# Two-layer recurrent decoder step on one core: second feed-forward's right operands formed inside the residual tiles, pools placed by hand, one store on another queue

## Chip, cores, metric

The kernel runs on one core of a Trainium2 chip. The metric is the device time of one execution in microseconds; several executions are timed and their median is quoted. One more execution is profiled, and all rows below come from that one.

## What is computed

T = 1048 columns are carried through a trunk of two layers: 16 meta tokens and 1024 prompt tokens (one sequence, 1040 columns) and 8 single-token samples. The model width is 1024, so the residual is eight tiles of 128 x 1048. The reference, cut to what matters here:

```
for layer in range(2):
    x = even_mixer(x, ...) if layer == 0 else odd_mixer(x, ...)
    x = conv_ffn(x, buf_ffn[layer], norm_ffn[layer], w_up[layer], ..., w_down[layer])
y = rmsnorm(x, norm_final)

def conv_ffn(x, buf, norm, w_up, conv_w, conv_b, w_down):
    hup = rmsnorm(x, norm) @ w_up                  # 1024 -> 2 x 2816
    gate, val = jnp.split(hup, 2, axis=-1)
    gate, new_buf = causal_dwconv(gate, buf, conv_w, conv_b)   # width 3 over time
    return x + (jax.nn.gelu(gate) * val) @ w_down, new_buf     # 2816 -> 1024

def rmsnorm(x, g):
    return x * lax.rsqrt(jnp.mean(x * x, axis=-1, keepdims=True) + EPS) * g
```

The layer-0 mixer holds a gated linear attention and a diagonal state-space model. The layer-1 mixer is a Griffin block: a gelu branch times a gated linear recurrence, then an output projection of 1536 to 1024 that is added to x.

## The kernel before

Names: X0 to X7 are the residual tiles, HALF = 524 columns is half of one. PE does the matmuls, DVE, ACT and POOL are the three elementwise engines, SP issues most of the DMAs, POOL issues some. The kernel names its engines V (DVE), A (ACT) and P (POOL), and `tt` is a tensor_tensor on DVE unless P is given as its last argument. All queues run in order; a tile scheduler has laid out the order of each engine's instructions from the program text, and pools (stacks of tiles) decide which tile lies where in SBUF. A tile that is put where another lay waits for all readers and writers of that other.

**Split products.** Each float32 matmul operand is split into a high part (`split`: an ACT cast, L85) and a low part (the difference, on DVE, L45); a product is three matmuls (`mm3`, L128 to L130).

**Feed-forward, up.** `ffn_up` makes the two 2816-wide outputs in 22 inner tiles (`hidden(t)`, t = 0 to 21). It takes the 2 x 2 blocks (rows of x in two groups of four tiles, columns in two halves of 524) through seven products, not eight. The class `Seven` prepares the right operands from x times its gain: B11, B21, T2, T3, T1, B22 and T4, each for j = 0 to 3 (pair Xj, Xj+4). B11, B21 and B22 are quarters of x themselves (`plain`), and the other four are running differences (`sums`): ACT scales four quarters into tiles t of a pool of three (`t7`, L1013), POOL makes four subtractions per j, and each result is split. The left operands are sums of weight blocks (`sums(t)` in `ffn_up`): four blocks are loaded into wA (SP), POOL adds and subtracts them into wS, and the four results are split (whi, wlo). In `hidden(t)` the order of products is B11, B21, then T2, T3, T1, B22, T4. B11 and B21 of tiles 0 and 1 need no differences, and are made first for both (`first`), and between them and the rest stands `nx.finish()`, which sums the squares over partitions by an all-ones matmul (L147) and makes RB, the reciprocal root-mean-square. PSUM results go to p1 and R (B11 plus B21), u2 and u4 (kept partial sums), VL and C; VL is stored to DRAM as hdr[t] at L1186.

**Feed-forward, down.** `ffn_down` loads hdr[t] back as hr (L1216), splits it (ph, pl) and multiplies by the down weights in turns of 2, 4, 4, 4, 4, 4 inner tiles. A turn has 24 output pieces (8 tiles of x, 3 column ranges); each takes one of four PSUM banks ("bank") and is added to X by DVE, which frees the bank. At the start, X is loaded back from the DRAM copy xdn (L1224), issued by POOL.

**Layer-1 mixer.** Eight steps, two column halves by four groups G. The output projection `out` of one step runs in the next; the last one (`end`) adds to X column half 1 and calls `after` for each finished piece: sums of squares (`stats`, ACT squares, POOL adds into acc), the store of X to xdn (POOL queue), and for j = 0 to 2 the `sums` and B22. The operands B11 and B21 are made in the step half 1, G = 2; sums of j = 3 come after the mixer's pools are closed. Then `ffn_up(1)` begins.

So there are four places where one stage hands over to the next and PE depends on the other engines: mixer 0 to feed-forward 0 (about 535 to 575 us), up to down in layer 0 (994 to 1016), mixer 1 to feed-forward 1 (1756 to 1825), up to down in layer 1 (2244 to 2275).

The seven lines of `hidden` on which much below rests:

```
p1_ = [fp.tile([128, H2], F32, name="p1", bufs=2) for _ in range(2)]
R = fp.tile([128, 2 + T], F32, name="R", tag="rvc", bufs=5)
...
P.memset(R[:, 0:2], 0.0)
...
put(R, 2, p1, W)
...
prod(Z, ws2, "T2", False)
```

## Time and profile before

| what | value |
|---|---|
| median of 3 runs | 2531.71 us (2529.97 to 2532.13) |
| the profiled execution's own time | 2529.29 us |
| its span, first to last instruction | 2527.4 us |
| mean granted PE clock | 0.975 of full speed |
| busy share of the span | PE 94%, DVE 72%, ACT 45%, POOL 25% |

The span is what the views of the trace cover; 1.9 us of the profiled execution's time lie around it. PE's idle time, the span less its busy time, is 161.5 us in all; most of the kernel is a stretch in which PE never waits, and the idle time sits at the places listed above and inside the mixers.

### The profile page before, as it was taken

To read this page: it belongs to the slowest core of one execution; us is meant where nothing else is said; L and a number is where in the kernel's file an instruction comes from. 1 tells how busy PE (TensorE), PEld (TensorE's weight loads), DVE (VectorE), ACT (ScalarE), POOL (GpSimd) and SP (SyncE) were. 2 spreads that over 40 slices of the span, in tenths; PEclk is the share of its full clock that TensorE was granted. 3 is DMA by queue.
4 is the path that set the end of the run, shared out by engine and by line. 5 is a ranking of instruction groups with operands and counts; after the bars stand their busy time and mean duration, and the time that the engine had idled before them with its cause. 6 is when DMAs were issued, how large, how long until landed. Compare 5 with 4: busy or idle time off the path is not lost. (4 is left out here: it accounts for less than half of the span.)

```text
span 2527.4 us, 45164 instructions
## 1 busy us (share of the span) xinstructions
PE 2365.9 (94%) x17427; PEld 2318.0 (92%) x17427; DVE 1811.7 (72%) x3199; ACT 1133.1 (45%) x2258; POOL 620.4 (25%) x637
## 2 busy tenths in 40 slices
PE   7879999889999997999999999999499999979998
PEld 6778988879999997999999999999499999979998
DVE  9885788697777775654688778777777777755445
ACT  5124563654444443221575666657444444432123
POOL 4330000373333332000220001112644334310003
PEclk9999999999999999999999999999799999999999
DMA  3422325633333334332123333234233333343321
GB/s 116 106 70 79 101 79 168 205 112 114 120 122 121 119 115 146 125 106 90 46 85 96 99 100 93 87 101 136 99 116 120 114 114 114 119 169 115 96 85 69
DMA packets 200703, 277.08 MB, mean 110 GB/s; under 512 B 34312, under 2 KB 114136, under 8 KB 200488
## 3 DMA queue, kind: packets, MB, share of 16 engines
q1 hardware_dynamic: 189000, 254.43, 31.6%
q0 software_dynamic: 4736, 17.32, 1.9%
q10 hardware_dynamic: 6752, 2.45, 0.4%
q8 instruction: 137, 2.24, 0.4%
q14 instruction: 78, 0.64, 0.1%
HBM read 216.69 MB, written 51.43 MB: 106 GB/s over the span
## 5 line engine op out<-in xcount | busy, mean ns | idle before, releaser
L85 ACT CAST whi<-wraw 128x512 fp32r<-128x512 f32 (+2 forms) x449 | 261.3, 589 | 509.4 <-PE bank L129 384.8
L45 DVE TENSOR_TENSOR wlo<-wraw,whi 128x512 fp32r<-128x512 f32 (+2 forms) x448 | 330.3, 743 | 106.1 <-ACT whi L85 91.9
L45 DVE TENSOR_TENSOR X<-X,bank 128x352 f32<-128x352 f32 (+4 forms) x436 | 211.8, 489 | 226.2 <-PE bank L130 223.6
L128 PE MATMUL bank<-ph,whi 128*128 128x352 f32 (+1 forms) x960 | 311.1, 325 | 28.1 <-ACT ph L85 24.6
L129 PE MATMUL bank<-pl,whi 128*128 128x352 f32 (+1 forms) x960 | 311.5, 324 | 0.0
L130 PE MATMUL bank<-ph,wlo 128*128 128x352 f32 (+1 forms) x960 | 310.3, 323 | 0.0
L45 POOL TENSOR_TENSOR acc<-acc,sq 128x352 f32<-128x352 f32 (+3 forms) x105 | 112.9, 1082 | 591.9 <-ACT sq L143 589.3
L45 DVE TENSOR_TENSOR wlo<-wS,whi 128x512 fp32r<-128x512 f32 x176 | 126.7, 721 | 141.0 <-ACT whi L85 140.6
L85 ACT CAST whi<-wS 128x512 fp32r<-128x512 f32 x176 | 109.0, 621 | 251.1 <-PE p L129 143.7
L128 PEld LDWEIGHTS bank<-ph,whi 128*128 128x128 f32 x960 | 181.9, 190 | 29.9 <-ACT ph L85 25.5
L129 PEld LDWEIGHTS bank<-pl,whi 128*128 128x128 f32 x960 | 181.9, 189 | 1.3 <-DVE pl L45 0.5
L130 PEld LDWEIGHTS bank<-ph,wlo 128*128 128x128 f32 x960 | 182.0, 190 | 0.0
L45 POOL TENSOR_TENSOR wS<-wA 128x512 f32<-128x512 f32 x88 | 150.8, 1714 | 119.7 <-DVE wlo L45 112.3
L128 PE MATMUL bank<-H,whi 128*128 128x352 f32 (+1 forms) x480 | 160.8, 338 | 19.0 <-DVE X L45 9.0
L129 PE MATMUL bank<-L,whi 128*128 128x352 f32 (+1 forms) x480 | 160.2, 336 | 6.8 <-DVE L L48 6.6
L130 PE MATMUL bank<-H,wlo 128*128 128x352 f32 (+1 forms) x480 | 157.9, 331 | 0.9 <-DVE wlo L45 0.9
L45 POOL TENSOR_TENSOR wS<-wA,wS 128x512 f32<-128x512 f32 x44 | 57.5, 1308 | 372.6 <-DVE wlo L45 372.6
L48 DVE SCALAR_TENSOR_TENSOR C<-R,CV,C 128x1040 f32<-128x1040 f32 x88 | 132.9, 1510 | 0.6 <-ACT C L1176 0.6
L128 PEld LDWEIGHTS bank<-H,whi 128*128 128x128 f32 x480 | 93.1, 195 | 23.3 <-DVE X L45 9.4
L128 PE MATMUL bank<-ryh,whi 128*128 128x262 f32 x372 | 105.5, 286 | 3.1 <-ACT ryh L85 1.8
L129 PE MATMUL bank<-ryl,whi 128*128 128x262 f32 x372 | 105.6, 285 | 0.6 <-DVE ryl L45 0.6
L130 PE MATMUL bank<-ryh,wlo 128*128 128x262 f32 x372 | 105.2, 284 | 0.0
(807 smaller groups left out, 8229.3 us busy)
## 6 DMA issues: line engine op xcount, KB each, us to landing
wA<-in_w_up SPq DMA_DIRECT2D x176, 256.0 KB, 2.7
wraw<-in_w_up SPq DMA_DIRECT2D x132, 256.0 KB, 4.8
wraw<-in_w_in SPq DMA_DIRECT2D x96, 256.0 KB, 2.6
hdr<-VL SPq DMA_DIRECT2D x44, 524.0 KB, 4.0
hr<-hdr SPq DMA_DIRECT2D x44, 524.0 KB, 3.9
wraw<-in_w_dn SPq DMA_DIRECT2D x80, 256.0 KB, 2.6
wraw<-in_w_out SPq DMA_DIRECT2D x48, 256.0 KB, 2.7
xdn<-X POOLq DMA_DIRECT2D x16, 524.0 KB, 3.8
```

What stands on the lines that cost most here:

```text
L45: return (eng or V).tensor_tensor(out=o, in0=x, in1=y, op=op)
L48: V.scalar_tensor_tensor(out=o, in0=x, scalar=s, in1=y, op0=op0, op1=op1)
L85: A.copy(out=h, in_=x)
L128: PE.matmul(out=out, lhsT=wh, rhs=xh, start=first and i == 0, stop=False, **kw)
L129: PE.matmul(out=out, lhsT=wh, rhs=xl, start=False, stop=False, **kw)
L130: PE.matmul(out=out, lhsT=wl, rhs=xh, start=False, stop=last and i == n - 1, **kw)
```

## The change

1. `Seven` has two new methods. `gained` scales a half of X in place by its gain (ACT). `sums_in` forms the differences in place in Xj and Xj+4: two subtractions per j on POOL and two on DVE where `sums` had four on POOL, and five splits. Layer 1 uses these; the pool t7 is gone, and j = 3 is treated like the others.
2. In the last three steps but one of mixer 1, a new `before(m)` does for the first column half of tile m: stats, its store to xdn, `gained`, and the split that makes B11 or B21. `after` now stores and scales only the second half, then calls `sums_in`. Since `gained` overwrites X, it waits until the store of that half has landed.
3. The pools of `ffn_up` are laid out by `places`, R, VL and C have two buffers each where they shared five, and `nx.finish()` stands inside `hidden(0)` behind the T2 product.
4. The store of the last inner tile, hdr[21], is issued by POOL, not by SP.
5. In `ffn_down`, every other piece of the first turn takes its PSUM bank from the ring "aux", so eight banks serve it; some tiles are padded.

```
...
-                    self.o[k, j] = tuple(pool.tile([128, HALF], F32R, name=f"{k}{j}{x}") for x in "hl")
+                    hl = pool.tile([128, 2, HALF], F32R, name=f"{k}{j}")
+                    self.o[k, j] = hl[:, 0], hl[:, 1]
...
+        def gained(self, m, x):
+            A.activation(out=x, in_=x, func=ACTF.Copy, scale=CV[:, self.gain + m:self.gain + m + 1])
+        def sums_in(self, j, x1, x2):
+            a0, a1 = slice(0, HALF), slice(HALF, T)
+            tt(x1[:, a0], x1[:, a1], x1[:, a0], SUB, P)
+            split(*self.o["B22", j], x2[:, a1])
+            tt(x1[:, a1], x2[:, a1], x1[:, a1], SUB, P)
+            tt(x2[:, a1], x2[:, a1], x1[:, a0], SUB)
+            split(*self.o["T2", j], x2[:, a1])
+            split(*self.o["T3", j], x1[:, a1])
+            split(*self.o["T1", j], x1[:, a0])
+            tt(x2[:, a0], x2[:, a0], x2[:, a1], SUB)
+            split(*self.o["T4", j], x2[:, a0])
...
-        es, fp = open_pool(f"ffn{layer}")
+        es = ExitStack()
+        at = {}
+        def places(name, *tags):
+            at.update(dict.fromkeys(tags, es.enter_context(tc.tile_pool(name=f"{name}{layer}", bufs=1, reuse_waits="tile"))))
+        if fw:
+            at.update(wA=fw, wS=fw)
+            places("fa", "p1", "R")
+            places("fb", "VL", "C", "u2", "u4", "FC")
+        else:
+            places("fa", "wA")
+            places("fb", "VL", "u2")
+            places("fc", "wS")
+            places("fd", "C", "u4", "FC")
+            places("fe", "p1", "R")
+        fp = at["FC"]
...
-                r[i, k] = (fw or fp).tile([128, 512], F32, name="wA", bufs=4)
+                r[i, k] = at["wA"].tile([128, 512], F32, name="wA", bufs=4)
-            s1, s2, s3, s4_ = ((fw or fp).tile([128, 512], F32, name="wS", bufs=3) for _ in range(4))
+            s1, s2, s3, s4_ = (at["wS"].tile([128, 512], F32, name="wS", bufs=3) for _ in range(4))
...
-            p1_ = [fp.tile([128, H2], F32, name="p1", bufs=2) for _ in range(2)]
-            R = fp.tile([128, 2 + T], F32, name="R", tag="rvc", bufs=5)
+            p1_ = [at["p1"].tile([128, H2], F32, name="p1", bufs=2) for _ in range(2)]
+            R = at["R"].tile([128, 2 + T], F32, name="R", bufs=2)
...
-                    u = p1_[c] if nm == "p1" else fp.tile([128, H2], F32, name=nm, bufs=2)
+                    u = p1_[c] if nm == "p1" else at[nm].tile([128, H2], F32, name=nm, bufs=2)
...
-            VL = fp.tile([128, T], F32, name="VL", tag="rvc", bufs=5)
+            VL = at["VL"].tile([128, T], F32, name="VL", bufs=2)
+            if t == 0:
+                nx.finish()
...
-            C = fp.tile([128, T], F32, name="C", tag="rvc", bufs=5)
+            C = at["C"].tile([128, T], F32, name="C", bufs=2)
...
-            nc.sync.dma_start(out=hdr[t], in_=VL)
+            (P if t == NFF - 1 else nc.sync).dma_start(out=hdr[t], in_=VL)
-        nx.finish()
...
-        def place(t):
-            return tuple(dq.tile([128, T], F32R, name=f"{x}{t % 6}") for x in ("ph", "pl"))
-        places = {t: place(t) for t in ((2, 3) if nxt else (2, 3, 4, 5))}
+        def place(t, pad=0):
+            hl = (dq.tile([128, T + pad], F32R, name=f"{x}{t % 6}") for x in ("ph", "pl"))
+            return tuple(x[:, :T] for x in hl)
+        places = {t: place(t, 136 if nxt and t == 3 else 0) for t in ((2, 3) if nxt else (2, 3, 4, 5))}
-            dl = [tuple(dq.tile([128, 512], F32R, name=f"{x}{m}") for x in ("wh", "wl")) for m in range(8)]
+            dl = [tuple(dq.tile([128, 512 if m < 7 else 768], F32R, name=f"{x}{m}") for x in ("wh", "wl")) for m in range(8)]
...
-            for m, (c0, n) in order:
+            for i, (m, (c0, n)) in enumerate(order):
-                p = bank()
+                p = ps.tile([128, 512], F32, name="p", tag="aux", bufs=4) if t0 == 0 and i % 2 else bank()
...
-            P.dma_start(out=xdn[m], in_=X[m])
-            if 4 <= m < 7:
-                nxt.sums(m - 4, X[m - 4], X[m], t7)
-                nxt.plain(m - 4, X[m], "B22")
+            P.dma_start(out=xdn[m][:, HALF:], in_=X[m][:, HALF:])
+            nxt.gained(m, X[m][:, HALF:])
+            if m >= 4:
+                nxt.sums_in(m - 4, X[m - 4], X[m])
+    def before(m):
+        for c0, n in HCH:
+            stats(m, c0, n)
+        P.dma_start(out=xdn[m][:, :HALF], in_=X[m][:, :HALF])
+        nxt.gained(m, X[m][:, :HALF])
+        op = "B11" if m < 4 else "B21"
+        nxt.o[op, m % 4] = halves(hlp, 0, m)
+        split(*nxt.o[op, m % 4], X[m][:, :HALF])
...
-    early = [(m, c0, n) for m in range(8) for c0, n in HCH]
...
-        if half and G == 2:
-            for i, op in enumerate(("B11", "B21")):
-                for j in range(4):
-                    nxt.o[op, j] = halves(hlp, 0, 4 * i + j)
-                    nxt.plain(j, X[4 * i + j], op)
-                for _ in range(6):
-                    if early:
-                        stats(*early.pop(0))
+                for m in range(3 * G, min(3 * G + 3, 8)):
+                    before(m)
-    t7s, t7 = open_pool("t7")
-    nxt.new(range(3), ("T1", "B22", "T4"), bm)
+    nxt.new(range(4), ("T1", "B22", "T4"), bm)
-    t7s.close()
-    bls, bl = open_pool("bl1", "right")
+    xps.close()
-    nx.new((3,), ("T1", "B22", "T4"), bl)
-    t7s, t7 = open_pool("t7")
-    nx.sums(3, X[3], X[7], t7)
-    nx.plain(3, X[7], "B22")
-    t7s.close()
-    xps.close()
-    bls.close()
```

What the change moves, as each engine's instructions stand in program order. Numbers in names tell tiles apart; b0 to b3 are T2, b4 to b7 T3 of j = 0 to 3, and l and h the low and high part.

DVE at the hand-over to feed-forward 1, before: the last splits of the differences, then the first work on R, then the weight sums' low parts. t_20851 is a tile of t7.

```order
L45 TENSOR_TENSOR T13l<-t_20851,T13h 128x524
L48 SCALAR_TENSOR_TENSOR B223l<-X_11447,CV,B223h 128x524
L45 TENSOR_TENSOR T43l<-t_20851,T43h 128x524
L45 TENSOR_TENSOR R<-p_20880,p 128x262
L45 TENSOR_TENSOR R<-p_20881,p 128x262
L45 TENSOR_TENSOR R<-p_20952,p 128x262
L45 TENSOR_TENSOR R<-R,RB 128x524
L45 TENSOR_TENSOR R<-p_20953,p 128x262
L156 RECIPROCAL RB<-RB 128x262 x2
L45 TENSOR_TENSOR wlo<-wS,whi 128x512 x3
```

The same place after; X_11423 is X7, X_11419 X3, T_20458 and T_20466 are T1 and T4 of j = 3, B_20462 is B22 of j = 3.

```order
L45 TENSOR_TENSOR B_20462<-X_11423,B_20462 128x524
L45 TENSOR_TENSOR T_20465<-X_11422,T_20465 128x524
L45 TENSOR_TENSOR X_11423<-X_11423,X_11419 128x524
L45 TENSOR_TENSOR b7l<-X_11419,b7h 128x524
L45 TENSOR_TENSOR T_20458<-X_11419,T_20458 128x524
L45 TENSOR_TENSOR b3l<-X_11423,b3h 128x524
L45 TENSOR_TENSOR X_11423<-X_11423 128x524
L156 RECIPROCAL RB<-RB 128x262
L45 TENSOR_TENSOR T_20466<-X_11423,T_20466 128x524
L156 RECIPROCAL RB<-RB 128x262
L45 TENSOR_TENSOR R<-R,RB 128x524 x2
L45 TENSOR_TENSOR wlo<-wS,whi 128x512 x4
```

The four pieces of R now stand further up, between the splits; subtractions into X7 have come in; both products of R with RB stand in front of the weight splits.

ACT at the same place after: the last cast of a difference, and then two first taps of the convolution, C, ahead of the casts of the weight sums (before, the casts of the sums came first).

```order
L85 CAST T43_20466<-X7_11423 128x524
L1213 ACTIVATE C_21175<-R_20843,CV_69 128x524
L1213 ACTIVATE C_21364<-R_20915,CV_69 128x524
L85 CAST whi_21000<-wS_20994 128x512
```

SP where feed-forward 0 goes from up to down, before:

```order
L113 DMA wraw_11727<-in_w_dn 128x2x128
L113 DMA wraw_11793<-in_w_dn 128x4x128
L1186 DMA hdr21_5007<-VL_11277 128x1048
L1216 DMA hr_11487<-hdr0_4986 128x1048
L1216 DMA hr_11497<-hdr1_4987 128x1048
```

POOL at that place after, whose queue held only the loads of X there before:

```order
L1223 DMA hdr21_5007<-VL_11252 128x1048
L1262 DMA X0_11416<-xdn0_4978 128x1048
L1262 DMA X1_11417<-xdn1_4979 128x1048
L1262 DMA X2_11418<-xdn2_4980 128x1048
```

The store has left SP, where the two loads of hr now follow the weights directly, and stands on POOL ahead of all loads of X. Layer 1 has the same orders at its place.

## Rows read from the trace of the kernel before

**Rows 1.** View 1 of the page, busy time by engine.

```profile
PE 2365.9 (94%) x17427; PEld 2318.0 (92%) x17427; DVE 1811.7 (72%) x3199; ACT 1133.1 (45%) x2258; POOL 620.4 (25%) x637
```

**Rows 2.** PE's waits by releaser, 1745 to 1830 us: total, times, longest.

```profile
PE p L147 <- DVE R L45: 28.0, 1, 28.0
PE bank L128 <- ACT whi L85: 3.6, 1, 3.6
```

**Rows 3.** Timeline of DVE, 1742 to 1808: start, duration, instruction, idle before.

```profile
1761.57 0.41 DVE L45 TENSOR_TENSOR X<-X,bank 128x262 f32<-128x262 f32 x1
1762.52 0.69 DVE L45 TENSOR_TENSOR T10l<-t,T10h 128x524 fp32r<-128x524 f32 x1
1770.62 8.18 DVE L45 TENSOR_TENSOR T11l<-t,T11h 128x524 fp32r<-128x524 f32 x1 [3.14 <-ACT T11h L85]
1795.24 0.70 DVE L45 TENSOR_TENSOR T43l<-t,T43h 128x524 fp32r<-128x524 f32 x1 [2.07 <-ACT T43h L85]
1798.19 3.44 DVE L156 RECIPROCAL RB<-RB 128x262 f32<-128x262 f32 x2
```

**Rows 4.** Timeline of POOL, the same window.

```profile
1770.58 5.02 POOL L45 TENSOR_TENSOR t<-t,t 128x524 f32<-128x524 f32 x4
```

**Rows 5.** Groups of POOL by shape, 1745 to 1802: busy, mean ns, idle before.

```profile
L45 POOL TENSOR_TENSOR t<-t,t 128x524 f32<-128x524 f32 x16 | 22.0, 1383 | 8.9 <-ACT t L1013 8.7
```

**Rows 6.** Groups of ACT by shape, the same stretch.

```profile
L1013 ACT ACTIVATE t<-X,CV 128x524 f32<-128x524 f32 x15 | 10.6, 728 | 4.5 <-DVE T11l L45 2.6 <-DVE b4l L45 1.5 <-DVE T10l L45 0.2
```

**Rows 7.** Timeline of ACT, the same window.

```profile
1801.48 0.62 ACT L85 CAST whi<-wS 128x512 fp32r<-128x512 f32 x1 [2.44 <-POOL wS L45]
```

**Rows 8.** PE's waits, 990 to 1020.

```profile
PE bank L128 <- ACT ph L85: 13.7, 2, 13.1
```

**Rows 9.** Timeline of SP's queue, 990 to 1004.

```profile
993.77 4.17 SPq L113 DMA_DIRECT2D wraw<-in_w_dn  x2
998.71 0.34 SPq L1186 DMA_DIRECT2D hdr<-VL  x1
999.10 1.57 SPq L1216 DMA_DIRECT2D hr<-hdr  x2
```

**Rows 10.** Timeline of POOL, 988 to 1010.

```profile
992.37 1.68 POOL L1224 DMA_DIRECT2D X<-xdn  x3
```

**Rows 11.** Timeline of ACT, 998 to 1010.

```profile
1006.95 1.25 ACT L85 CAST ph<-hr 128x352 fp32r<-128x352 f32 x3 [9.66 <-DMA hr<-hdr]
```

**Rows 12.** Windows: length, busy (PE, PEld, DVE, ACT, POOL), PEclk, DMA share, GB/s.

```profile
994.00:999.00 5.00, 0.34 (x3) 0.13 (x2) 4.68 (x7) 1.57 (x3) 0.59 (x2) 0.99 0.96 331
999.00:1004.00 5.00, 0.00 (x0) 0.00 (x0) 0.00 (x0) 0.00 (x0) 1.07 (x2) 0.50 1.05 397
```

**Rows 13.** Page, DMA issues: size, median us from issue to landing.

```profile
hr<-hdr SPq DMA_DIRECT2D x44, 524.0 KB, 3.9
xdn<-X POOLq DMA_DIRECT2D x16, 524.0 KB, 3.8
```

**Rows 14.** PE's waits, 2240 to 2275.

```profile
PE bank L128 <- ACT ph L85: 10.9, 1, 10.9
PE bank L128 <- DVE X L45: 3.1, 2, 2.0
```

**Rows 15.** Timeline of SP's queue, 2240 to 2256.

```profile
2242.90 2.40 SPq L113 DMA_DIRECT2D wraw<-in_w_dn  x2
2249.06 1.36 SPq L1216 DMA_DIRECT2D hr<-hdr  x2
```

**Rows 16.** Timeline of POOL, 2240 to 2262.

```profile
2253.45 3.19 POOL L1224 DMA_DIRECT2D X<-xdn  x6 [6.25 <-DMA hdr<-VL]
```

**Rows 17.** Timeline of ACT, 2248 to 2258.

```profile
2254.36 2.53 ACT L85 CAST ph<-hr 128x352 fp32r<-128x352 f32 x6 [6.99 <-DMA hr<-hdr]
```

**Rows 18.** PE's waits, 530 to 580.

```profile
PE p L147 <- DVE R L45: 1.0, 1, 1.0
```

**Rows 19.** PE's waits, 1500 to 1756.

```profile
PE bank L128 <- DVE rgg L45: 10.1, 4, 4.0
```

## The prediction

> **What bounds the kernel now.** I read the page's busy times first: PE is busy 2365.9 of 2527.4 us [rows 1]. The change leaves the number of matmuls as it is, so it can only work on the 161.5 us in which PE is idle, or add to them. Next I asked for PE's waits by stretch, because an average over the span does not say which of them last. Four places carry what the change touches.
>
> The largest is the hand-over from mixer 1 to feed-forward 1: PE waits 28.0 us in one piece and 3.6 us soon after [rows 2]. The reader is to see that the releaser of the 28.0, a DVE write of R, was no long job itself. It stood in DVE's queue behind the splits of the differences, the last of which, T43l, ran at 1795.24 and took 0.70, so ended at 1795.94 [rows 3]; R and p1 lie where the pool of those differences lay, and are free only then. PE's real restart is that of the T2 product, which needs the cast whi of the first weight sum: 1801.48 plus 0.62 is 1802.1 [rows 7]. From T43l's end to there is 6.2 us.
>
> The next two are the turns from up to down, 13.7 us in layer 0 [rows 8], and 10.9 plus 3.1 us in layer 1 [rows 14]. The releaser named is the cast ph of the first hr tile, and the cast itself waited for the load of hr [rows 11, 17]. So there the DMA ends last. The start of feed-forward 0 has 1.0 us of a kind that the change can reach [rows 18], and the second half of mixer 1 has 10.1 us of waits for a DVE product [rows 19].
>
> **The change, part by part.** The sum is in five terms.
>
> A, the hand-over to feed-forward 1. First what DVE and POOL share. T11l needed 8.18 us where T10l, the same shape, needed 0.69 [rows 3]; in that time POOL ran four subtractions back to back in 5.02 us, so 1.26 each [rows 4], and T11l ended only once POOL paused. A DVE add with one operand in PSUM kept its 0.41 us [rows 3] while POOL was at work too. I therefore treat a DVE operation with both operands in SBUF and a POOL operation as taking turns. The Trainium skill has the rule, on the page "SBUF — State Buffer", section "Who interferes with whom": a DVE instruction with two SBUF inputs and a GpSimd instruction that reads SBUF cannot run at once, the loser is blocked entirely, and one with a single SBUF input is free. By that rule the trace agrees (8.18 against 0.69), and moving a subtraction from POOL to DVE does not put it beside the others.
>
> Before, POOL has 16 subtractions in this stretch [rows 5]; its additions of squares stay. The change takes eight subtractions off POOL, 8 x 1.26 = 10.1 us, and puts eight on DVE, 8 x 0.69 = 5.5. On a shared budget that saves 4.6. Were the two engines independent, POOL would save the whole 10.1 and DVE would have room for its 5.5. But now more stands on DVE in front of T43l: four writes of R from PSUM, 4 x 0.41 = 1.6, and the first of two reciprocals, half of 3.44 = 1.7 [rows 3]. That is 3.3 back. Behind T43l stand now the second reciprocal 1.7, two products of R with RB (one SBUF shape of 524 columns each, as T10l) 1.4, two first taps C on ACT (nearest row 0.73 for that shape [rows 6]) 1.5, and the cast whi 0.6: 5.2, with hand-overs some 5.4, against 6.2 before. Saved 0.8. POOL's waits of 8.7 us in all for ACT's scaled quarters [rows 5] should shrink, since the first halves of X are now scaled within the mixer; I let the longer chain use that up, for each j now goes from POOL to DVE to ACT and back to DVE in one fixed order. The weight sums lie elsewhere now and should be ready before PE asks, but ACT's casts of them stand behind the two C, so they gain nothing. A is -4.6 + 3.3 - 0.8, so about -2. Bounds: if no DVE operation is caught as T11l was, 7.5 less, so -9.5. If each of the eight new subtractions on DVE waits for one POOL operation in front, 8 x 1.26 = 10 more, so +8.
>
> B, up to down in layer 0. SP's weight loads end at 993.77 + 4.17 = 997.9; then came the store of hdr[21] at 998.71, which had to wait for VL, and the load of hr[0] at 999.10 [rows 9]. Its data were cast at 1006.95 [rows 11], 7.9 us after the issue, where the median of these loads is 3.9 [rows 13], because from 992.37 on POOL had the loads of X in the same DMA engines [rows 10], which moved 397 GB/s with a share of 1.05 while no compute engine but POOL's issuing did anything [rows 12]. After, hr[0] is next on SP at 998.0, and every load of X stands behind the store of hdr[21] on POOL, which waits for the same VL (998.7). With the median landing hr[0] is there at 1001.9 instead of 1006.95: -5. Bounds: -6 if it lands in the time of a lone load, -2 if it still takes 7 us. Here the Trainium skill has something against it: the page "DMA: Bandwidth & Descriptors", section "Queues, rings and completion order", says that a DMA engine takes turns between queue rows packet by packet, so the store and the loads of X on the other queue still share with hr. By that rule hr's last part, from about 999, moves at half of the 397 GB/s; half a megabyte then takes 2.6 instead of 1.3 us, and B would be -3.7. The loads of X start some 6.5 us later than before. What hides this is the bank ring: with four banks PE would stand at its fifth piece until X0 was there, with eight at its ninth. Without that cover the term would be near zero.
>
> C, up to down in layer 1. SP is free for hr at 2242.90 + 2.40 = 2245.3 instead of 2249.06 [rows 15], 3.8 earlier, and two loads of X are no longer ahead of it; with a landing of 3.9 it is there at 2249.2. Before, the cast on it started at 2254.36 [rows 17]: -5.2. Most loads of X come at 2253.45 as before, since they wait for the store of hdr[21] to land [rows 16]. The 3.1 us of waits for additions to X [rows 14] are what four more banks can cover, up to all of it. C is -8; bounds -8.5 and -3 (the landing as slow as before, 2254.36 less 2249.06, so 5.3 us, which leaves 3.8, and 0.8 us of more bank waits).
>
> D, feed-forward 0's start: the all-ones matmul stands behind T2 now, so its 1.0 us wait for R [rows 18] goes: -1, bounds 0 and -2.
>
> E, mixer 1's second half: eight scalings at 0.73 [rows 6] are 5.8 us more for ACT, plus eight store issues and squares that come together with them; the splits of B11 and B21 move from one step to behind three recurrences. PE waits for DVE there already (10.1 us [rows 19]). The cover is PE's own work, some 60 us a step. I take +1, bounds -2 and +6, as ACT's 5.8 would cost it all if none were covered.
>
> The stretches inside `ffn_up` and `ffn_down` in which PE never waits stay as they are. The sum: -2 - 5 - 8 - 1 + 1 = -15. The profiled execution took 2529.3 in its own time, so 2514.3; the median of the runs is 2.4 above that execution, and on its scale the forecast is 2531.7 - 15 = 2516.7, rounded to 2517.
>
> **Rivals.**
>
> 1. The hand-over gains much: DVE and POOL mesh better with fewer POOL runs of four, so nothing is caught as T11l was. For it: POOL has half the subtractions, and never four in a row. Against it: the chain through three engines has more steps. A is -9.5, the sum -22.5, the time 2509.
> 2. The hand-over loses: the in-place chain costs a POOL operation at each of the eight DVE subtractions. For it: each such subtraction reads what POOL has just written. Against it: other splits stand between them. A is +8, the sum -5, the time 2527.
> 3. The turns gain little: hr shares its bandwidth with the store and X so that it lands as slowly as before, and the later X takes away what the banks give. For it: 397 GB/s is what the engines move at most in these rows. Against it: the loads of X are issued after hr. B is -2 and C -3, the sum -7, the time 2525.
> 4. Slower: the scaling in place must wait for the store of its half to land, and ACT, in order, stands there with all its casts behind it. Eight stores of 3.8 us [rows 13] are 30 us; if 20 of them come onto the path, the sum is +5, the time 2537. It decides from 15 us on, half of it. For it: the store and the scaling of the same tile are only a few instructions apart. Against it: the last addition to X comes only at 1761.57 [rows 3], so the stores are spread over the end of the output projection, and ACT has squares and casts of other tiles in between.
>
> **How the numbers follow.** Forecast 0.45, rival 1 0.20, rival 2 0.15, rival 3 0.11, rival 4 0.09. About 0.2%, 5 us, is what a measurement of this kernel can tell from no change. The forecast and rival 1 are faster (0.65); rival 2 straddles the bound at -5 and rival 3 lies just beyond it at -7, so I count 0.07 and 0.08 of them as faster and the rest as the same, with 0.02 of rival 4 the same as well: faster 0.80, same 0.13, slower 0.07. The range runs from a little below rival 1 (its A with E at its best, 2507) to just above rival 2 (2529), which leaves out rival 4 and some of the tails.
>
> **What will show it.** A: T43l's place and the T2 product's start; right if PE restarts between 1797 and 1803 on the old scale. B and C: the load of hr right behind the weight loads, its landing time, and ph's wait under 9 and 6 us; no wait of PE on X in layer 1. E: PE's waits on DVE in mixer 1's second half within 3 us of 10.1. The forecast is wrong if POOL's and DVE's operations stretch each other by more than before, or if ACT shows waits for stores.

## The result

The changed kernel takes 2517.16 us (median of 4 runs, 2510.99 to 2520.11); the kernel before, timed beside it, 2531.92. The ratio is 0.9939, with a 95% interval of 0.9919 to 0.9959, so the change saves 10 to 21 us. The forecast was 2517. The profiled execution took 2510.99 in its own time and its span is 2509.2 us, the fastest of the four, so it stands 18.3 us below before's profile where the medians stand 14.8 apart.

The busy times of the page, to be read against [rows 1]. PE's idle time is now 138.0 us where it was 161.5, but PE is also 5.3 us longer busy with the same 17427 matmuls. That was in no term of the forecast; part of it comes back below as PE's pace.

```profile
PE 2371.2 (95%) x17427; PEld 2324.9 (93%) x17427; DVE 1803.9 (72%) x3207; ACT 1124.8 (45%) x2258; POOL 625.7 (25%) x639
```

**The hand-over to feed-forward 1.** PE's waits from 1700 to 1830, against [rows 2]: 28.0 and 3.6 have become 16.1 and 9.2. The wait for R is gone, and the all-ones matmul waits for the sums of squares only.

```profile
PE bank L128 <- ACT whi L85: 16.1, 1, 16.1
PE p L147 <- POOL acc L45: 9.2, 1, 9.2
```

The timeline of DVE, against [rows 3]. The first line is the last addition to X; T<-X,T at 1783.09 is T43l, `b3l` the last low part of T2.

```profile
1750.68 0.41 DVE L45 TENSOR_TENSOR X<-X,bank 128x262 f32<-128x262 f32 x1
...
1771.56 1.78 DVE L45 TENSOR_TENSOR X<-X 128x524 f32<-128x524 f32 x1
1773.27 1.77 DVE L45 TENSOR_TENSOR b2l<-X,b2h 128x524 fp32r<-128x524 f32 x1
...
1780.16 0.69 DVE L45 TENSOR_TENSOR b3l<-X,b3h 128x524 fp32r<-128x524 f32 x1
...
1783.09 0.97 DVE L45 TENSOR_TENSOR T<-X,T 128x524 fp32r<-128x524 f32 x1
1783.98 1.78 DVE L156 RECIPROCAL RB<-RB 128x262 f32<-128x262 f32 x1
1785.68 1.24 DVE L45 TENSOR_TENSOR R<-R,RB 128x524 f32<-128x524 f32 x2
```

And ACT behind it, against [rows 7]:

```profile
1786.41 1.54 ACT L1213 ACTIVATE C<-R,CV 128x524 f32<-128x524 f32 x2 [4.28 <-DVE R L45]
1787.86 1.64 ACT L85 CAST whi<-wS 128x512 fp32r<-128x512 f32 x3
```

No DVE operation was caught for 8.18 us any more; with POOL at work beside them they took 1.2 to 1.8 us, and 0.69 alone. The chain behind T43l (reciprocal, R, C, whi) is there as forecast.

**From up to down.** PE's waits of layer 0 (980 to 1020), against [rows 8], and of layer 1 (2200 to 2280), against [rows 14]; the waits for X are gone.

```profile
PE bank L128 <- ACT ph L85: 10.4, 1, 10.4
```

```profile
PE bank L128 <- ACT ph L85: 6.1, 1, 6.1
```

SP, POOL and ACT in layer 0, against [rows 9 to 11]. The loads of hr follow the weights directly, and the cast of the first tile starts 6.3 us after the issue, with the second tile's right behind it.

```profile
992.20 4.04 SPq L113 DMA_DIRECT2D wraw<-in_w_dn  x2
996.29 0.97 SPq L1254 DMA_DIRECT2D hr<-hdr  x2
```

```profile
997.28 0.60 POOL L1223 DMA_DIRECT2D hdr<-VL  x1 [6.51 <-DVE VL L45]
997.87 3.73 POOL L1262 DMA_DIRECT2D X<-xdn  x7
```

```profile
1002.55 2.53 ACT L85 CAST ph<-hr 128x352 fp32r<-128x352 f32 x6 [6.96 <-DMA hr<-hdr]
```

In layer 1 the same, against [rows 15 to 17]: 4.3 us from issue to cast, and most loads of X wait for the store, as before.

```profile
2234.73 8.05 SPq L1254 DMA_DIRECT2D hr<-hdr  x4
```

```profile
2242.56 3.19 POOL L1262 DMA_DIRECT2D X<-xdn  x6 [2.58 <-DMA hdr<-VL]
```

```profile
2239.04 1.25 ACT L85 CAST ph<-hr 128x352 fp32r<-128x352 f32 x3 [2.30 <-DMA hr<-hdr]
```

**PE's own pace.** Windows of PE inside the two up stages, in which it never waits: length, busy time with the number of matmuls, clock, DMA share, GB/s. Before:

```profile
1860.00:2190.00 330.00, 330.00 (x2720) 1.00 0.35 116
640.00:940.00 300.00, 300.00 (x2450) 1.00 0.34 114
```

After:

```profile
1860.00:2190.00 330.00, 330.00 (x2690) 1.00 0.35 116
640.00:940.00 300.00, 300.00 (x2462) 1.00 0.34 115
```

The clock is full in all four. In the second stage PE does 30 matmuls fewer in the same time: 122.7 ns each where it was 121.3. An inner tile has 168 of them and the stage 22 tiles, so this costs 1.35 ns x 3696 = 5.0 us. In the first stage it is faster (122.4 to 121.9 ns, some 2 us); but so is e2 below, in which nothing of this stage is changed, so this gain is not shown to come from the change.

**Where the time went, piece by piece.** The trace lists the start of each matmul. The table has, for each kernel that follows, how much longer than in before's profile each piece took, from the first matmul to the last, cut at matmuls 2950, 3300, 6690, 6960, 12050, 12420, 15780 and 16050 (in before at 519.8, 577.7, 993.1, 1053.7, 1746.1, 1829.4, 2237.4 and 2295.7 us).

```
                      mixer 0     D   up 0     B  down 0+mixer 1     A  up 1     C  down 1
after                     2.1  -1.9   -1.9  -5.7            -0.3  -7.5   4.5  -7.9     0.1
e1_after_again            5.5  -1.4   -1.9  -5.3             0.4  -7.6   4.5  -7.2     0.0
e2_turns_only             4.5  -0.1   -2.6  -4.1             4.9   0.5   0.0  -7.0     0.0
e4_without_turns          4.1  -1.3   -1.9   1.6             0.2  -7.4   4.5  -0.8     0.0
e6_casts_first            0.3  -1.4   -1.9  -3.7             2.0 -12.1   4.5  -6.4     0.1
e7_all_dve                4.5  -1.7   -1.9  -3.7             2.2 -13.4   4.5  -6.9     0.1
e8_all_pool               2.1  -1.9   -1.9  -4.0            -0.7  -7.2   4.5  -6.7     0.1
e9_hl_joined              3.3   0.0   -1.9  -2.2            -1.3   0.6  -1.1   0.3     0.1
e10_pools_only            5.1  -1.3   -2.6   1.8             4.7  -3.1   4.5  -1.5     0.0
e11_casts_first_dve       0.9  -1.9   -1.9  -6.2             0.8 -12.2   4.5  -5.9     0.1
e12_ones_twice            2.0  -1.9   -1.9  -4.0             2.0  -7.4   4.5  -7.2     0.0
e13_ones_ahead            2.7  -1.9   -1.9  -6.5             1.1  -7.8   4.5  -7.1     0.1
e14_pools_swapped         3.6  -1.4   -1.9  -6.4             3.5  -7.5   4.5  -7.6     0.0
```

A column repeats itself where a cause is at work. Two do not: mixer 0, which no kernel here changes, lies 0.3 to 5.5 above the one profile of before (3.1 in the mean), and the column with mixer 1 scatters from -1.3 to 4.9 with or without the change. I take both as scatter between executions. In the kernels without parts 4 and 5 (e4, e9, e10) B scatters from -2.2 to 1.8 and C from -1.5 to 0.3, so I read no difference under some 4 us in B or 2 in C from one profile.

### The profile page after: what moved, and what is told of

It is laid out like the page before. It is cut to its first block, busy times and chain, and to the rows that moved or that the text cites. A ratio compares the mean times of both kernels' runs of the same rounds, so it can differ in the third digit from the quotient of the medians.

```text
span 2509.2 us, 45220 instructions
## 1 busy us (share of the span) xinstructions
PE 2371.2 (95%) x17427; PEld 2324.9 (93%) x17427; DVE 1803.9 (72%) x3207; ACT 1124.8 (45%) x2258; POOL 625.7 (25%) x639
## 5 line engine op out<-in xcount | busy, mean ns | idle before, releaser
L45 DVE TENSOR_TENSOR X<-X,bank 128x352 f32<-128x352 f32 (+4 forms) x412 | 198.9, 487 | 219.4 <-PE bank L130 216.8
L128 PE MATMUL bank<-ph,whi 128*128 128x352 f32 (+1 forms) x912 | 294.2, 323 | 16.6 <-ACT ph L85 16.6
L129 PE MATMUL bank<-pl,whi 128*128 128x352 f32 (+1 forms) x912 | 294.8, 323 | 0.0
L130 PE MATMUL bank<-ph,wlo 128*128 128x352 f32 (+1 forms) x912 | 294.5, 323 | 0.0
L128 PEld LDWEIGHTS bank<-ph,whi 128*128 128x128 f32 x912 | 172.0, 189 | 17.0 <-ACT ph L85 17.0
L130 PEld LDWEIGHTS bank<-ph,wlo 128*128 128x128 f32 x912 | 172.1, 189 | 0.0
L128 PE MATMUL bank<-B,whi 128*128 128x262 f32 x528 | 151.7, 287 | 0.0
L130 PE MATMUL bank<-B,wlo 128*128 128x262 f32 x528 | 151.1, 286 | 0.0
L129 PE MATMUL bank<-B,whi 128*128 128x262 f32 x528 | 150.7, 285 | 0.0
L129 PE MATMUL p<-T,whi 128*128 128x262 f32 x528 | 150.4, 285 | 0.0
L128 PE MATMUL bank<-T,whi 128*128 128x262 f32 x528 | 150.4, 285 | 0.0
```

The lines of the kernel that those rows point to most:

```text
L45: return (eng or V).tensor_tensor(out=o, in0=x, in1=y, op=op)
L128: PE.matmul(out=out, lhsT=wh, rhs=xh, start=first and i == 0, stop=False, **kw)
L129: PE.matmul(out=out, lhsT=wh, rhs=xl, start=False, stop=False, **kw)
L130: PE.matmul(out=out, lhsT=wl, rhs=xh, start=False, stop=last and i == n - 1, **kw)
```

## The experiments

All ratios are to the kernel before, timed on the same chip in the same session, with 95% intervals.

**e1_after_again**, the changed kernel once more, unaltered.

> The changed kernel once more, unaltered, for its spread and for one thing that the trace showed and the forecast did not have: in the up stage of feed-forward 1 PE, never waiting, needed 20.62 us per inner tile where the kernel before needed 20.40, in layer 0 20.50 against 20.58. If this pace belongs to the program (places of tiles, the waits in its instructions), this execution shows 20.6 and 20.5 again; if it belongs to the single execution, at least one of the two moves by 0.1 or more. Time in both cases within 2517 plus or minus 4 us.

Measured: 2516.37, ratio 0.9936 (0.9919 to 0.9952). Every piece but mixer 0 returns within 0.7 us, and the two windows of the up stages hold 2690 and 2462 matmuls again. So the changed kernel's pace belongs to the program and not to the execution. Of the kernel before there is one profile; e2 repeats its 2720 matmuls in the second stage, but not its 2450 in the first (2466).

**e2_turns_only**, the kernel before with parts 4 and 5 of the change.

```
-            nc.sync.dma_start(out=hdr[t], in_=VL)
+            (P if t == NFF - 1 else nc.sync).dma_start(out=hdr[t], in_=VL)
-                p = bank()
+                p = ps.tile(..., tag="aux", bufs=4) if t0 == 0 and i % 2 else bank()
```

> The kernel before with two of the five parts: the last store on POOL's queue, and eight banks in the first turn of ffn_down. My theory: the two turns from up to down are independent of the rest, so this gains the 5.8 and 7.8 us that the two traces show there: 13 us, 2518 to 2520. Rival, that the turns gain only together with the new pool layout (hr and X wait for other places here): less than 8 us, 2524 or more.

Measured: 2522.74, 0.9961 (0.9947 to 0.9976), which is 6 to 13 us saved: less than the 13 expected, more than the rival's 8 by the ratio (9.9). B is -4.1 and C -7.0, most of the full kernel's, so the turns do not need the new pool layout.

**e4_without_turns**, the changed kernel with those two parts taken out (the lines above with + and - exchanged).

> The changed kernel without those two parts: the last store is back on SP, four banks in the first turn; in-place differences, early first halves and pool layout are kept. My theory: what these give at the hand-over (5.8 us in the trace) and in mixer 1 (about 2) is nearly used up by the slower pace in the up stage of feed-forward 1 (4.4), so this stands 1 to 4 us under the kernel before, at 2528 to 2531. Rival, that the new layout also helps the turns: 2522 or less.

Measured: 2528.41, 0.9983 (0.9972 to 0.9993). B and C are gone (1.6 and -0.8; its waits there are 17.2, and 10.3 with 2.7 for X), A and D stay. By the ratios the two halves save 9.9 and 4.3 us, together 14.2, where the whole saves 16.2 in the same session (e1), which is within their intervals.

**e6_casts_first**, the changed kernel with the reciprocals, the products of R with RB and the first taps C of the first two tiles queued behind the first three weight splits.

```
+                with behind(t, 1):
+                    nx.finish()
...
+            with behind(t, 1):
+                tt(R[:, 2:2 + HALF], R[:, 2:2 + HALF], RB[:, :HALF], MUL)
...
+              with behind(t, 0):
                 (the first taps C, on ACT)
```

> The changed kernel with one more order: in the first two inner tiles of feed-forward 1 the reciprocals, the products of R with RB and the first taps C stand behind the first three weight splits on DVE and ACT. My theory of the hand-over: the difference chain ends with T43 at 1784 us of the changed kernel's trace, and what stands between it and PE's restart at 1788.4 is only order, so PE restarts 4 to 6 us earlier and the time falls by as much, to 2511 to 2514. Rival, that DVE and POOL as shared hands are what binds there: what is moved behind comes back as a later wait of PE within the same stretch, and the time stays within 2 us of the changed kernel's.

Measured: 2513.38, 0.9919 (0.9905 to 0.9933). A is -12.1. PE's waits in the hand-over, by its own line numbers:

```profile
PE bank L127 <- ACT whi L85: 10.3, 1, 10.3
PE p L146 <- POOL acc L45: 9.2, 1, 9.2
PE bank L127 <- ACT u L1182: 1.1, 1, 1.1
```

So the order on DVE and ACT behind T43l, which the forecast had priced at 5.2 us plus hand-overs, does hold PE for about 5 us by the trace: 5.8 us less at the first wait, 1.1 of it back at a new one. By the medians of the same session it is 3.0 us (2516.37 to 2513.38), and the two intervals overlap.

**e7_all_dve** and **e8_all_pool**: all four differences of each j on DVE, or all four on POOL; the changed kernel has two and two.

```
-            tt(x1[:, a0], x1[:, a1], x1[:, a0], SUB, P)
+            tt(x1[:, a0], x1[:, a1], x1[:, a0], SUB)
-            tt(x1[:, a1], x2[:, a1], x1[:, a1], SUB, P)
+            tt(x1[:, a1], x2[:, a1], x1[:, a1], SUB)
```

> The kernel after, with all four differences of each j on DVE (eight of the 128x524 subtractions in the hand-over move from POOL to DVE). My theory: DVE operations with both operands in SBUF and POOL operations take turns, so what counts is the sum of both, and the move saves 8 x (1.26 - 0.69) = 4.6 us of it; the DVE operations of 1.75 us near the end of the hand-over become 0.7 where POOL has no subtraction beside them. Expected 3 to 5 us less than the kernel after, so about 2512 to 2514. Rival: the two engines work independently and DVE, which has the longer queue there, is the bound; 8 x 0.69 = 5.5 us more on it give 2518 to 2522.

> The kernel after, with all four differences of each j on POOL, as in the kernel before, but still formed in place. My theory of turns: the sum of both engines' work rises by 8 x (1.26 - 0.69) = 4.6 us, so 2519 to 2522, with DVE splits of over 3 us where POOL has several subtractions in a row. Rival, independent engines: DVE has 5.5 us less to do, so 2511 to 2515.

Measured: 2510.49, 0.9910 (0.9892 to 0.9929), and 2514.28, 0.9931 (0.9913 to 0.9948). On DVE the gain came as priced or a little above (A -13.4 against -7.5; from the last addition to X to T43l's end 28.9 us where after has 33.4). DVE's operations ran back to back at 0.69, and POOL's first weight sum, with nothing changed in it, stood until they were done; the timeline of DVE and of POOL in e7:

```profile
1781.26 0.69 DVE L45 TENSOR_TENSOR b7l<-X,b7h 128x524 fp32r<-128x524 f32 x1
1781.87 0.69 DVE L45 TENSOR_TENSOR X<-X 128x524 f32<-128x524 f32 x1
1782.49 0.69 DVE L45 TENSOR_TENSOR b3l<-X,b3h 128x524 fp32r<-128x524 f32 x1
```

```profile
1772.81 11.50 POOL L45 TENSOR_TENSOR wS<-wA 128x512 f32<-128x512 f32 x1 [6.23 <-DVE T L45]
1784.38 1.26 POOL L45 TENSOR_TENSOR wS<-wS,wA 128x512 f32<-128x512 f32 x1
```

On POOL the loss that I had priced at 4.6 us did not come (A -7.2; 34.7 us to T43l's end), and the time lies in the range of the rival, independent engines; but independent they are not, as DVE's operations beside POOL took up to 1.9 us there too. Windows from the last addition to X to the first cast whi say why the loss stayed away: length; busy PE, PEld, DVE, ACT, POOL; clock; DMA. Before, after, e7 and e8:

```profile
1761.57:1801.48 39.91, 8.95 (x61) 7.83 (x60) 31.55 (x28) 20.94 (x39) 26.75 (x26) 0.65 0.19 69
```

```profile
1750.68:1787.86 37.18, 12.51 (x88) 10.89 (x86) 35.30 (x37) 18.39 (x38) 27.54 (x26) 0.68 0.24 80
```

```profile
1757.29:1790.13 32.84, 11.38 (x91) 10.90 (x89) 32.08 (x45) 18.25 (x35) 24.35 (x19) 0.75 0.26 88
```

```profile
1751.81:1790.22 38.41, 12.58 (x88) 10.89 (x86) 32.73 (x29) 19.05 (x37) 35.92 (x31) 0.66 0.20 65
```

Busy time includes the time in which one engine stands for the other. After, DVE is full (35.30 of 37.18) and POOL has room; in e8 POOL is full (35.92 of 38.41), and DVE has room. From after to e8 the end moves by 1.2 us, so it goes with the fuller queue and not with the sum of both. That DVE and POOL take turns is borne out by e7; that the sum of their work sets the end, as I had reckoned, is not.

**e11_casts_first_dve**, e6 and e7 together.

> Both improvements of the hand-over together: all four differences of each j on DVE, and the reciprocals, the products of R with RB and the first two taps behind the first three weight splits. Apart, each took some 6 us off the hand-over of the kernel after by the trace (5.9 and 6.0). My theory: the first is worth DVE's and POOL's lost time, the second takes PE's restart off the tail behind T43l, so they add in part: with all differences on DVE the weight sums on POOL are late (the first ran 11.50 us and the third ended 1.1 us after T43l's last split), so of the second's 5 us some 2 to 4 are left. Expected 2506 to 2509, against 2510.5 with the differences on DVE alone. Rival: the weight sums on POOL, starved by DVE, are the next gate and nothing is added: 2510 to 2512.

Measured: 2509.14, 0.9902 (0.9883 to 0.9921), the fastest here, but not to be told from e7. By the median it is on the edge of both; by the trace the rival is right: A is -12.2, no more than either alone. PE restarts earlier and then waits a second time, for what comes behind the late weight sums:

```profile
PE bank L127 <- ACT whi L85: 18.0, 1, 18.0
PE bank L127 <- ACT u L1182: 3.0, 1, 3.0
```

**e9_hl_joined** and **e10_pools_only**, two parts of the change alone on the kernel before: the one line that puts high and low part of an operand side by side, and all of part 3 (pools, and the all-ones matmul behind T2).

```
-                    self.o[k, j] = tuple(pool.tile([128, HALF], F32R, name=f"{k}{j}{x}") for x in "hl")
+                    hl = pool.tile([128, 2, HALF], F32R, name=f"{k}{j}")
+                    self.o[k, j] = hl[:, 0], hl[:, 1]
```

> The kernel before with one line of the change alone: high and low part of a right operand lie in one tile, side by side, not in two. It asks where the slower pace of PE in the second up stage of the kernel after (20.63 us per inner tile, 20.40 before, and 20.49 against 20.59 in the first) comes from. If from where the right operands lie: 20.6 in the second stage and some 5 us more there, so about 2535 in all, or less by what the first stage gains. If from the pools of the up stage or anything else: 20.4 in the second stage as before and a time within 2 us of before.

> The kernel before with the new layout of the pools of the up stages and the all-ones matmul behind the T2 product, and nothing else of the change. Theory: the start of the first up stage gains its 1 to 2 us, and the hand-over into the second gains little, since the differences there still go through tiles of their own, with four subtractions in a row on POOL: 2527 to 2531. Rival: the hand-over's gain comes from the layout and not from forming the differences in place: 2523 to 2526. For the pace of PE: 20.63 us per inner tile in the second up stage if it comes from where the pools of that stage lie, 20.40 if not.

Measured: 2528.13, 0.9989 (0.9976 to 1.0003), and 2531.68, 1.0000 (0.9986 to 1.0015). The window of the second up stage, e9 and then e10:

```profile
1860.00:2190.00 330.00, 330.00 (x2728) 1.00 0.36 118
```

```profile
1860.00:2190.00 330.00, 330.00 (x2690) 1.00 0.35 116
```

The slow pace comes with part 3 and not with the operands' new form; e9 is even faster than before. It is not where PE's own operands lie, either: in e10 all 3698 matmuls of that stage read and write the same places of SBUF and PSUM as in before, and they are slow. e10 also splits A: part 3 alone gives -3.1 of the -7.5, and parts 1 and 2 together the rest. The time, 2531.68, is a little above the 2527 to 2531 expected. In e10, with the differences in tiles of their own, the long DVE operation is back:

```profile
1778.16 8.18 DVE L45 TENSOR_TENSOR T11l<-t,T11h 128x524 fp32r<-128x524 f32 x1 [3.14 <-ACT T11h L85]
```

So part 3 by itself saves nothing: what it gives at D and A, the second up stage takes back.

**e12_ones_twice, e13_ones_ahead, e14_pools_swapped**, three variants of the changed kernel that look for the cause of the pace: the all-ones matmuls of the second layer twice; `nx.finish()` written ahead of T2 again in the second layer (in PE's own order its matmuls stand ahead of T2 there in all these kernels); two pools exchanged. The last edit does not do what its expectation says. It stands in the branch `if fw:`, and only the call `ffn_up(0, nx, fw)` takes that branch, so it exchanges the two pools of the first up stage and leaves those of the second as they were.

```
+        if twice:
+            colsum(p[:, :n], acc[:, :n])
...
-            if t == 0:
+            if t == 0 and not layer:
                 nx.finish()
...
+            places("fb", "VL", "C", "u2", "u4", "FC")
             places("fa", "p1", "R")
-            places("fb", "VL", "C", "u2", "u4", "FC")
```

> The kernel after with the all-ones matmuls of the second layer done twice: four more matmuls on PE ahead of the second up stage, nothing else. It asks whether PE's pace in that stage (20.63 us per inner tile after, 20.40 before) hangs on where the stage's instructions stand in PE's stream. If so: a pace clearly other than 20.63, such as 20.40, and some 5 us less; if not: 20.63 as after. The hand-over loses at most 1 us.

> The kernel after with the finishing of the sums of squares in the second layer written ahead of the T2 product again, as before; it changes which banks of the ring its two matmuls and the first two tiles take, and the order on the other engines, not PE's order. If the pace of the second up stage comes from how its first tiles take banks: 20.40 us per inner tile; if from the layout of its pools: 20.63. The hand-over stays within 2 us of after.

> The kernel after with the two pools of the second up stage in the other order (VL, C, u2, u4 below, p1 and R above); PE's instructions and their operands stay where they are. It asks whether the places of these buffers, which PE never reads, set PE's pace in that stage. If so: another pace than 20.63 us per inner tile; if not, 20.63. The hand-over may lose some us, since R and p1 now lie where places come free at another time; 2514 to 2522 in all.

Measured: 2515.73 and 2512.51 (one run each), and 2515.41, 0.9925 (0.9905 to 0.9945). All three keep the slow pace, +4.5 us in the table. For e12 and e13 this says that what they change is not the cause by itself. e14 does not test the pools of the second stage; in the first stage, whose pools it does exchange, it has the 2462 matmuls of after, so there the order of the two does not matter. It settles something else. All the other slow kernels have one wait instruction less than before in PE's stream ahead of the second stage, 191 where before has 192; e14 has 192 and is as slow.

## Why the prediction was right

The forecast of the sum held, -15 against -14.8 by the medians, but that the two lie so near is luck: the terms err to both sides, as follows.

- **C**, -8 forecast: -7.9 and -7.2 in the two profiles of the changed kernel, -7.0 with parts 4 and 5 alone, -0.8 without them. Right by its own steps: hr 3.8 us earlier on SP, landing 4.3 us where 3.9 was taken, no wait for X left; ph's wait is 6.1 where under 6 was asked. Rival 3 is refuted here.
- **B**, -5 forecast: -5.7 and -5.3. The size came out with the help of PE's clock; the landing on which it rested was wrong. hr landed 6.3 us after its issue and not 3.9, as the first of seven loads of X was issued only 1.6 us behind it; in layer 1, with two loads of X there, it took 4.3. PE's wait fell from 13.7 to 10.4, by 3.3, and not under 9 as the forecast asked. The Trainium skill says on the page "DMA: Bandwidth & Descriptors", section "Queues, rings and completion order", that a DMA engine takes turns packet by packet between the queue rows that it has work for. The trace agrees in direction, and the -3.7 that the forecast had by that rule is the nearer figure. The rest is the clock: before, it stood at 0.50, the lower of its two levels, until about 1016, 8.5 us after PE's first matmul of the turn (1007.5); after, until about 1006, 3.1 us after it (1003.1). At 0.50 PE does 9 matmuls in 2 us and at 1.00 it does 15, so 5.4 us less at 0.50 are worth some 2.2. The windows of PE, before and after:

```profile
1012.00:1014.00 2.00, 2.00 (x9) 0.50 0.77 262
1014.00:1016.00 2.00, 2.00 (x9) 0.51 0.13 50
1016.00:1018.00 2.00, 2.00 (x15) 1.00 0.43 131
```

```profile
1004.00:1006.00 2.00, 2.00 (x8) 0.50 1.03 421
1006.00:1008.00 2.00, 2.00 (x14) 0.96 1.02 421
```

That part is chance. Of the ten profiles with parts 4 and 5, five have the clock back 3.1 to 4.5 us after the first matmul of this turn, and a B of -5.3 to -6.5; the other five have it back after 6.4 to 9.7 us, and a B of -3.7 to -4.1. Beside before's 8.5, the change itself is worth about -4 here.
- **A**, -2 forecast: -7.5 and -7.6. What it priced came out about right; the step that failed is what it put at nothing, the time ahead of the last addition to X and the time behind PE's restart. Follow the trace from PE's last matmul of the output projection (1756.5 in before, 1748.9 after). From there to the last addition to X it was 5.0 us and is 1.8: -3.2, in no term. From there to T43l's end it was 34.4 and is 33.4: -1.0, where the forecast had -4.6 + 3.3 = -1.3. From there to T2's first matmul (1802.1 and 1788.5) it was 6.2 and is 4.5: -1.8, where it had -0.8. Behind that, another -1.5, in no term; among it is a stop of PE of 1.2 us that before has at 1815.6. On the old scale PE restarts at 1796.2, earlier than the 1797 to 1803 that the forecast asked. In before a weight split and `b4l`, both beside work of POOL, stood ahead of the last addition to X on DVE (at 1761.57 [rows 3]); after, `b4l` stands behind it:

```profile
1756.61 3.02 DVE L45 TENSOR_TENSOR wlo<-wraw,whi 128x512 fp32r<-128x512 f32 x1
1759.56 2.09 DVE L45 TENSOR_TENSOR b4l<-t,b4h 128x524 fp32r<-128x524 f32 x1
```

```profile
1751.85 1.26 DVE L45 TENSOR_TENSOR b4l<-X,b4h 128x524 fp32r<-128x524 f32 x1
```

e10, with part 3 alone, keeps the 5.0 us ahead of the addition and has 4.3 us behind T43l, so the 3.2 belong to parts 1 and 2 and the shorter tail to part 3, whose weight sums the forecast had gaining nothing. Rival 1 saw the 8.18 us go, and it went with the differences in tiles of their own (e10 has it still); but as other DVE operations beside POOL now took 1.2 to 1.8 us, this made the stretch only 1.0 us shorter, not 7.5. The order behind T43l was read rightly (e6 takes 4.6 us out of A). Of the 4.6 for the shared budget, e7 shows 4.5 and e8, the other way, 1.3, so the -1.3 came so near the -1.0 partly by chance. Rival 2, a POOL operation's time at each DVE subtraction, is refuted: the term is not +8, and e8, with every subtraction on POOL, is no worse.
- **D**, -1 forecast: -1.9 and -1.4; the wait for R is gone. **E**, +1 forecast: PE's waits for DVE there are 9.5 us where they were 10.1 [rows 19], and the column with mixer 1 shows nothing beyond its scatter.
- **Rival 4**, the scaling that waits for stores: ACT's scalings in place ran 729 ns each with 0.1 us of idle time before the fourteen that this group of ACT from 1480 to 1760 holds. Nothing waited for a store.

```profile
L1031 ACT ACTIVATE X<-X,CV 128x524 f32<-128x524 f32 x14 | 10.1, 729 | 0.1
```

- **The sentence that failed outright** is "The stretches inside `ffn_up` and `ffn_down` in which PE never waits stay as they are." The second up stage lost 4.5 us; the first shows 1.9 less, which e2 has too. As measured in after's profile, the five terms add up to -23.3 and with the two up stages to -20.7, where the medians differ by 14.8. What is left I put down to scatter against before's one profile: mixer 0, where nothing is changed, is 3.1 us longer in the mean of the thirteen others, and B's clock is worth some 2. The slower pace and this scatter are why a hand-over 5.5 us better than forecast did not carry the time to rival 1's 2509.

**What stays open** is why the pace differs. In the second up stage it is bound to part 3 of the change (e10). The places of PE's own operands do not set it (e10), nor do eight more of PE's records ahead of the stage (e12's four matmuls count twice), nor the place of `nx.finish()` in the program's text (e13), nor the one wait instruction less (e14). Not tried: where the other engines' pools of that stage lie, since e14 exchanged those of the first stage, and, apart from that, two buffers each for R, VL and C in place of five shared ones. In the first up stage, e2 left PE's instructions and their operands' places as before and yet has 20.45 us per inner tile where before's profile has 20.59; whether program or execution makes that difference is not shown.

## What to carry to other kernels

Price DVE and POOL in a hand-over by which of the two queues is full, blocked time included, and prefer DVE for dependent chains of short operations there; here, putting half of such a chain on POOL cost 6 us by the trace. Order what PE needs first ahead of everything that only later stages need; it was worth 3 us by the medians and 4.6 by the trace. The two gains did not add (e11). Begin the sum of a hand-over at PE's last matmul of the old stage, not at the work that is changed: 3.2 us lay ahead of it here. And compare the pace of PE in the stages that "do not change" between the two profiles before believing any sum of hand-overs: 1.35 ns per matmul outweighed two of the five terms (D and E).

## What the hardware showed that was not expected

- Two programs with the same matmuls at full clock differ in PE's pace by up to 1.4% (121.0 ns in e9, 122.7 ns after, for 262 columns), with the same count of matmuls when a program is run again (after and e1). In the second stage eleven profiles with part 3 hold 2690 or 2691 matmuls in 330 us, and the three without it 2720 or 2728.
- The mirror image of the 8.18 us: a POOL addition of 128x512 took 11.50 us beside an unbroken row of DVE operations of 0.69 with operands in SBUF, where the next one took 1.26. It looks as if the engine that always has its next operation ready keeps the other out.
- After a stall, PE's clock comes back at very different times. In the turn of layer 0, after stalls of 8 to 18 us, it was back at full 3.1 to 9.7 us after PE's first matmul in the fourteen profiles, and differently in kernels that do the same there. Gaps in PE's work are not the whole of it: PE was busy 3.92 of the 4.5 us from its restart to 1012 in before (8.5 us) and without a gap in after (3.1 us), but in layer 1 it had no gap until the clock was back in either, and it was the other way round: 3.5 us in before, 5.6 after.
